# Remainders of the first part's weight tiles: 512 columns by DVE, the other 512 by GpSimd

## The chip, the cores and the metric

The kernel runs on one core of one Trainium2 chip. What is measured is the device time of one execution in microseconds (us). Of the core's engines the text uses these names: PE is TensorE's matmul stream and PEld its weight loads, DVE is VectorE, ACT is ScalarE, POOL is GpSimd, SP is the engine that issues most of the weight loads from memory. Each engine takes its instructions strictly in the order of its queue in this program, and waits on semaphores for the others.

## What is computed

One block of a streaming encoder on 256 tokens of 2048 channels, all in float32. Cut to what matters:

```
h = rmsnorm(x, norm1_g) * (1 + scale1) + shift1          # shift1, scale1, ... = silu(c) @ ada_w + ada_b
proj = h @ w_in                                           # 2048 -> 9216 columns
u, v, q, k, vb, gates = split(proj)
y_a = spatial_gating(gelu(u), gelu(v)) @ w_branch_a       # layer norm, 8 groups of 128 x 128 block-causal mixing
y_b = band_attention(q, k, vb, rel_bias) @ w_branch_b     # 16 heads
x = x + gate1 * ((sig(gates_a) * y_a + sig(gates_b) * y_b) @ w_out)
h = rmsnorm(x, norm2_g) * (1 + scale2) + shift2
x = x + gate2 * moe(h)                                    # 32 SwiGLU experts, top-1 group, top-2 experts in it
out = rmsnorm(x, final_g)
```

The first part is everything up to `w_out`: four dense products with weights (`w_in`, `w_branch_a`, `w_branch_b`, `w_out`). The second part is the 32 experts.

## The kernel before, in words

In the first part the matmuls run on the type fp32r, and precision is kept by splitting each operand in two: a high half, which is the value rounded to fp32r, and a remainder, which is the value less its high half. A product is then three matmuls: high by high, remainder of the activations by high, and high by remainder of the weights.

`run_steps` does that for one stretch of weight columns. It loads weights in pieces of 2 MB (`rw`, tiles r0 to r3) and works on **weight tiles** of 128 rows by `cw` columns (1024, but 512 in the last two stretches of `w_out`). For each weight tile, `prepare` makes the high half on ACT (L315, a cast into `wh`) and then the remainder on DVE (L316, `wl = src - wh`). Both lie in the tile W, which has two slots for high halves and two for remainders, used in turn. `prods` then gives PE the matmuls of that tile: for two token halves and two column halves of 512, L289 (high by high), L290 (activation remainder by `wh`) and L291 (activation high by `wl`), 12 in all. `push` writes the preparation of one tile ahead of the matmuls of the tile before, so that ACT and DVE work one tile ahead of PE. There are 192 weight tiles of 1024 columns and 32 of 512.

Order of the first part: `w_in` in four blocks of four row tiles (`BLOCKS`), each over five stretches of 1024 columns (20 weight tiles a block, `homes`); the partial sums of blocks 2 to 4 are added on DVE (L350, one operand from PSUM). Then the four gate stretches of `w_in` (16 tiles each), with attention and spatial gating as side work between the matmuls; then the branches (8 tiles each, four times); then `w_out` (16 tiles of 1024 columns, and 32 of 512).

Beside this, DVE computes the conditioning vectors without PE: `ada_block` and `ada_units` multiply rows of `ada_w` by a column of silu(c) and add them to an accumulator, one `scalar_tensor_tensor` of 128x1024 for each row tile (L204 in the blocks, L432 later; both inputs lie in SBUF). These steps are drawn by `next(with_ada)` in `prepare` and at each load, so that they stand in DVE's queue between the remainders; below they are the **conditioning steps**. There are 15 in each of the first three blocks' stretches, and 119 of L432 from the fourth block on.

GpSimd has little to do in the first part: a few memsets, loads of small vectors, and two tiny powers of the layer norm (L636). The order on each engine's queue is set by a scheduler, which places the instructions by its own estimates; `pin` marks those of the second part that it must leave in order. The second part streams 402 MB of expert weights through a ring of tiles, among them W, dC, dD and E of the first part.

Of the kernel before, what the change touches and what calls it, by code (L numbers as in the profile page):

```python
# [10 lines left out]
F32 = mybir.dt.float32  # L11
# [34 lines left out]
def hybrid_block(  # L46
# [25 lines left out]
    nc = tc.nc  # L72
# [10 lines left out]
    class Ring:  # L83
# [4 lines left out]
        def next(self):  # L88
            self.i = (self.i + 1) % len(self.tags)
            return self.tags[self.i - 1]  # L90
# [15 lines left out]
    def load(shape, src):  # L106
        t = raws.sb(shape)
        nc.sync.dma_start(out=t, in_=src)
        return t
# [6 lines left out]
    def push(prepare, products):  # L116
        prepare()
        if pending:
            pending.pop()()
        pending.append(products)  # L120
# [7 lines left out]
    def tick():  # L128
        for g in list(sides):
            if next(g, "end") == "end":  # L130
                sides.remove(g)
# [141 lines left out]
    def run_steps(lh, ll, w, k0, n, c0, evac, with_ada=None, cw=CW, after=None):  # L273

        nhf = cw // 512
        npc = 4096 // cw
        pt = []

        def prods(k, wh, wl, close):
            def f():  # L280
                if not pt:
                    pt.extend([bk.ps() for _ in range(nhf)] for _ in range(NT))
                for t in range(NT):
                    a = lh(k)[:, t * P : (t + 1) * P]
                    b = ll(k)[:, t * P : (t + 1) * P]
                    for hf in range(nhf):
                        cs = slice(hf * 512, (hf + 1) * 512)
                        o = pt[t][hf]
                        nc.tensor.matmul(o, a, wh[:, cs], start=(k == k0), stop=False)  # L289
                        nc.tensor.matmul(o, b, wh[:, cs], start=False, stop=False)  # L290
                        nc.tensor.matmul(o, a, wl[:, cs], start=False, stop=close)  # L291
                if close:
                    for t in range(NT):
                        for hf in range(nhf):
                            evac(t, hf, pt[t][hf])
                    if after is not None:
                        after()
                tick()

            return f  # L300

        for q in range(k0, k0 + n, npc):
            m = min(npc, k0 + n - q)
            rw = load([P, m, cw], w[q * P : (q + m) * P, c0 : c0 + cw].rearrange("(j p) n -> p j n", p=P))
            if with_ada is not None:
                next(with_ada, None)
            for jj in range(m):
                k = q + jj
                i2 = nsplit[0] % 2
                nsplit[0] += 1  # L310
                wh = split[:, i2, 0:cw]
                wl = split[:, 2 + i2, 0:cw]

                def prepare(wh=wh, wl=wl, src=rw[:, jj, :]):
                    nc.scalar.copy(wh, src)  # L315
                    nc.vector.tensor_sub(wl, src, wh.bitcast(F32))  # L316
                    if with_ada is not None:
                        next(with_ada, None)

                push(prepare, prods(k, wh, wl, k == k0 + n - 1))  # L320
# [658 lines left out]
    for j in range(-1, 4):  # L979
        for a in range(2):  # L980
            o, cs = pgate[a * CH : (a + 1) * CH, :], slice(a * 512, (a + 1) * 512)
# [570 lines left out]
```

## Time and profile before

| | us |
|---|---|
| median of 3 runs | 1694.18 (1693.98 to 1696.93) |
| the profiled execution, its own time | 1694.83 |
| its span (first to last profiled instruction) | 1693.1 |

| engine | busy, share of the span |
|---|---|
| PE | 1540.7 us, 91% |
| PEld | 858.7 us, 51% |
| DVE | 946.7 us, 56% |
| ACT | 483.5 us, 29% |
| POOL | 125.1 us, 7% |

Two stretches have to be told apart. The first part's weight tiles run on PE from 45 us to 698 us; after that the experts run to the end, with memory traffic near its ceiling throughout. The shares above are means over both. A busy PE says little, since ends of matmuls are modelled; the spacing of the weight tiles and the waits say more.

### The profile page before, as it was taken

What the parts mean: (1) busy time and instruction counts of PE and PEld (TensorE: products, weight loads), DVE (VectorE), ACT (ScalarE), POOL (GpSimd) and SP (SyncE); (2) the same over time, 40 slices, a digit from 0 to 9 for tenths busy, and PEclk for the clock granted to TensorE, in tenths of its full rate; (3) what the DMA queues carried; (4) which work ended last, traced back from release to release, by engine and by line L of the source; (5) the groups of instructions that cost most, each with busy time, mean ns of one, the idle gap of its engine ahead of it and who ended that gap; (6) DMA issues with size and microseconds to landing.
All of it is one profiled execution on the core that took longest, in us unless ns stands there. A gap on an engine that the chain in (4) does not pass through costs nothing. (4 is left out here: it accounts for less than half of the span.)

```text
span 1693.1 us, 18219 instructions
## 1 busy us (share of the span) xinstructions
PE 1540.7 (91%) x6709; PEld 858.7 (51%) x6709; DVE 946.7 (56%) x1320; ACT 483.5 (29%) x785; POOL 125.1 (7%) x377
## 2 busy tenths in 40 slices
PE   2999999999999999899998989989899898898996
PEld 1777778777887776543333323334233243332432
DVE  5789999998778979733432333323333333332334
ACT  4554345675444345331111111111111111111112
POOL 1000000000000000011110101001001010010101
PEclk9999999999999999899999999999999999999998
DMA  9988997797987886979999999999999999999996
GB/s 358 352 314 330 347 341 299 286 348 278 354 314 304 325 320 221 368 311 418 416 417 418 415 418 417 417 417 416 419 417 417 418 416 419 416 417 418 415 420 244
DMA packets 135359, 625.25 MB, mean 369 GB/s; under 512 B 5721, under 2 KB 5841, under 8 KB 101857
## 3 DMA queue, kind: packets, MB, share of 16 engines
q1 hardware_dynamic: 132832, 614.49, 91.3%
q10 hardware_dynamic: 992, 5.28, 0.8%
q0 software_dynamic: 1440, 4.27, 0.8%
q8 instruction: 55, 0.90, 0.2%
q14 instruction: 40, 0.32, 0.0%
HBM read 621.91 MB, written 2.10 MB: 369 GB/s over the span
## 5 line engine op out<-in xcount | busy, mean ns | idle before, releaser
L1203 PE MATMUL b<-r,e 128*64 128x512 f32 x1008 | 372.4, 640 | 43.8 <-DMA r<-in_w_dram 43.7
L1342 DVE TENSOR_TENSOR dB<-dB,b 128x512 f32<-128x512 f32 x248 | 153.6, 681 | 320.1 <-PE b L1340 320.1
L315 ACT CAST W<-r 128x1024 fp32r<-128x1024 f32 (+1 forms) x224 | 220.8, 987 | 326.5 <-PE b L290 291.8
L289 PE MATMUL b<-W,dC 128*128 128x512 f32 x704 | 284.2, 404 | 6.0 <-ACT dC L230 3.7
L316 DVE TENSOR_TENSOR W<-r,W 128x1024 fp32r<-128x1024 f32 (+1 forms) x224 | 255.3, 1145 | 60.5 <-ACT W L315 59.2
L290 PE MATMUL b<-W,dD 128*128 128x512 f32 x704 | 279.5, 397 | 0.0
L291 PE MATMUL b<-W,dC 128*128 128x512 f32 x704 | 266.9, 398 | 2.1 <-DVE W L316 1.9
L1332 ACT CAST f<-f 64x512 fp32r<-64x512 f32 x124 | 76.5, 617 | 578.9 <-DVE dB L1342 416.9
L1203 PEld LDWEIGHTS b<-r,e 128*64 128x64 f32 x1008 | 115.2, 146 | 227.6 <-issue 155.6
L432 DVE SCALAR_TENSOR_TENSOR f<-r,sc,f 128x1024 f32<-128x1024 f32 x119 | 152.2, 1280 | 4.4 <-DMA r<-in_ada_w_dram 3.6
L289 PEld LDWEIGHTS b<-W,dC 128*128 128x128 f32 x704 | 132.5, 188 | 41.5 <-ACT W L315 4.3
L291 PEld LDWEIGHTS b<-W,dC 128*128 128x128 f32 x704 | 131.2, 188 | 38.3 <-DVE W L316 7.1
L290 PEld LDWEIGHTS b<-W,dD 128*128 128x128 f32 x704 | 132.5, 188 | 30.4 <-issue 0.5
L1203 PE MATMUL b<-dC,e 128*64 128x512 f32 x272 | 123.5, 607 | 18.5 <-DMA dC<-in_w_dram 18.4
L1203 PE MATMUL b<-E,e 128*64 128x512 f32 x256 | 120.0, 624 | 20.2 <-DMA E<-in_w_dram 20.2
L1203 PE MATMUL b<-dD,e 128*64 128x512 f32 x256 | 124.8, 637 | 0.0
L1299 DVE TENSOR_TENSOR f2y<-f2y,b 128x256 f32<-128x256 f32 x31 | 13.1, 421 | 196.0 <-ACT f2y L1298 196.0
L1203 PE MATMUL b<-W,e 128*64 128x512 f32 x256 | 118.2, 609 | 0.6 <-POOL e L1216 0.5
L1308 PE MATMUL b<-r,f2y 128*64 128x512 f32 x512 | 114.7, 595 | 2.0 <-DVE f2y L1299 2.0
L1333 DVE TENSOR_TENSOR f<-f,f 64x512 fp32r<-64x512 f32 x124 | 85.1, 686 | 26.4 <-ACT f L1332 23.5
L1218 POOL COPY e<-a 128x64 f32 x256 | 67.5, 267 | 203.7 <-PE b L1203 189.9
L204 DVE SCALAR_TENSOR_TENSOR f<-r,sc,f 128x1024 f32<-128x1024 f32 x60 | 76.9, 1281 | 1.6 <-DMA r<-in_ada_w_dram 1.0
(313 smaller groups left out, 1473.6 us busy)
## 6 DMA issues: line engine op xcount, KB each, us to landing
r<-in_w_dram SPq DMA_DIRECT2D x92, 2048.0 KB, 28.2
r<-in_w_in_dram SPq DMA_DIRECT2D x36, 2048.0 KB, 8.1
r<-in_ada_w_dram SPq DMA_DIRECT2D x32, 2048.0 KB, 8.8
W<-in_w_dram SPq DMA_DIRECT2D x24, 2048.0 KB, 28.1
dC<-in_w_dram SPq DMA_DIRECT2D x23, 2048.0 KB, 28.3
dD<-in_w_dram SPq DMA_DIRECT2D x23, 2048.0 KB, 28.7
E<-in_w_dram SPq DMA_DIRECT2D x23, 2048.0 KB, 28.1
r<-in_ada_w_dram SPq DMA_DIRECT2D x32, 1024.0 KB, 10.1
```

The costliest lines, as they stand in the source:

```text
L204: nc.vector.scalar_tensor_tensor(out=acc, in0=rw[:, jj], scalar=sc[:, j : j + 1], in1=acc, op0=ALU.mult, op1=ALU.add,)
L289: nc.tensor.matmul(o, a, wh[:, cs], start=(k == k0), stop=False)
L290: nc.tensor.matmul(o, b, wh[:, cs], start=False, stop=False)
L291: nc.tensor.matmul(o, a, wl[:, cs], start=False, stop=close)
L315: nc.scalar.copy(wh, src)
L316: nc.vector.tensor_sub(wl, src, wh.bitcast(F32))
L432: nc.vector.scalar_tensor_tensor(out=acc, in0=rw[:, jj, :], scalar=sc[:, j : j + 1], in1=acc, op0=ALU.mult, op1=ALU.add,)
L1203: nc.tensor.matmul(pab[a * CH : (a + 1) * CH, :], xe[:, 8 * half + j, :], w[:, j // JQ, j % JQ, :], start=(half == 0 and j == 0), stop=(ha ...
L1308: nc.tensor.matmul(po[a * CH : (a + 1) * CH, :], act[:, j, :], w[:, j, a * 512 : (a + 1) * 512], start=(j == 0), stop=(j == 3),)
L1332: pin(nc.scalar.copy(oh[r, a, :], og[r, b, :]))
L1333: pin(nc.vector.tensor_sub(oh[o, a, :], og[r, b, :], oh[r, a, :].bitcast(F32)))
L1342: pin(nc.vector.tensor_add(xa[:, t, d0 : d0 + 512], xa[:, t, d0 : d0 + 512], pr))
```

## The change

Of the remainder of a weight tile, DVE keeps the first 512 columns, and GpSimd computes the 512 beside it. Tiles of 512 columns have nothing left for GpSimd.

```
                 def prepare(wh=wh, wl=wl, src=rw[:, jj, :]):
                     nc.scalar.copy(wh, src)
-                    nc.vector.tensor_sub(wl, src, wh.bitcast(F32))
+
+                    for eng, cs in ((nc.gpsimd, slice(512, cw)), (nc.vector, slice(0, 512))):
+                        if cs.start < cw:
+                            eng.tensor_sub(wl[:, cs], src[:, cs], wh[:, cs].bitcast(F32))
                     if with_ada is not None:
                         next(with_ada, None)
```

In the changed program later lines stand three lines lower: L319 is the remainder (L316 before) on either engine, L353 the adding of partial sums (L350 before), L204 is the conditioning step in both. The scheduler places the queues anew. Three places:

**DVE, second block, two stretches of `w_in`.** Before: W is the remainder, f the conditioning step, E and e the adding of partial sums.

```order
L316 TENSOR_TENSOR W_63<-r_86_678,W_63 128x1024
L350 TENSOR_TENSOR E_228<-E_228,b_83_633 128x512
L350 TENSOR_TENSOR E_228<-E_228,b_84_634 128x512
L350 TENSOR_TENSOR E_228<-E_228,b_85_635 128x512
L316 TENSOR_TENSOR W_63<-r_86_678,W_63 128x1024
L204 SCALAR_TENSOR_TENSOR f_80_606<-r_87_680,sc_92,f_80_606 128x1024
L316 TENSOR_TENSOR W_63<-r_86_678,W_63 128x1024
L204 SCALAR_TENSOR_TENSOR f_80_606<-r_87_680,sc_92,f_80_606 128x1024
L316 TENSOR_TENSOR W_63<-r_86_678,W_63 128x1024
L204 SCALAR_TENSOR_TENSOR f_80_606<-r_87_680,sc_92,f_80_606 128x1024
```

The same place in the changed program:

```order
L319 TENSOR_TENSOR W_63<-r_86_702,W_63 128x512
L353 TENSOR_TENSOR E_228<-E_228,b_83_655 128x512
L353 TENSOR_TENSOR E_228<-E_228,b_84_656 128x512
L353 TENSOR_TENSOR E_228<-E_228,b_85_657 128x512
L319 TENSOR_TENSOR W_63<-r_86_702,W_63 128x512
L204 SCALAR_TENSOR_TENSOR f_80_626<-r_87_704,sc_92,f_80_626 128x1024 x2
L319 TENSOR_TENSOR W_63<-r_86_702,W_63 128x512
L204 SCALAR_TENSOR_TENSOR f_80_626<-r_87_704,sc_92,f_80_626 128x1024 x2
L319 TENSOR_TENSOR W_63<-r_86_702,W_63 128x512
```

The remainders are half as wide, and the conditioning steps stand in pairs between two remainders instead of one by one.

**POOL, from the start of the weight tiles.** Before, after the memset L268, come a memset (L400) and small loads of the fourth block:

```order
L241 TENSOR_TENSOR rs_n_21_105<-ve_n_20_103,mhalf_71 128x2
L268 MEMSET f_30_157 64x8x64
L400 MEMSET f_326_2821 128x1024
L401 DMA f_326_2821<-in_ada_b_dram 1x16x64
L498 DMA dB_1378<-in_gmlp_ln_g_dram 128x1024
```

In the changed program:

```order
L241 TENSOR_TENSOR rs_n_21_105<-ve_n_20_103,mhalf_71 128x2
L268 MEMSET f_30_157 64x8x64
L319 TENSOR_TENSOR W_63<-r_46_233,W_63 128x512 x4
L319 TENSOR_TENSOR W_63<-r_53_295,W_63 128x512 x4
L319 TENSOR_TENSOR W_63<-r_59_372,W_63 128x512 x4
L319 TENSOR_TENSOR W_63<-r_65_449,W_63 128x512 x4
```

GpSimd's queue, empty there before, now holds one subtraction of 128x512 for each of the 192 tiles of 1024 columns, and its memsets and loads stand between them.

**PE, third block.** Before, the matmuls of the second weight tile of a stretch: the four that need the remainder (L291) come last.

```order
L289 MATMUL b_121_1092<-W_63,dC_97 128x512
L290 MATMUL b_121_1092<-W_63,dD_98 128x512
L289 MATMUL b_122_1093<-W_63,dC_97 128x512
L290 MATMUL b_122_1093<-W_63,dD_98 128x512
L289 MATMUL b_123_1094<-W_63,dC_97 128x512
L290 MATMUL b_123_1094<-W_63,dD_98 128x512
L289 MATMUL b_124_1095<-W_63,dC_97 128x512
L290 MATMUL b_124_1095<-W_63,dD_98 128x512
L291 MATMUL b_121_1092<-W_63,dC_97 128x512
L291 MATMUL b_122_1093<-W_63,dC_97 128x512
L291 MATMUL b_123_1094<-W_63,dC_97 128x512
L291 MATMUL b_124_1095<-W_63,dC_97 128x512
```

The same tile in the changed program:

```order
L289 MATMUL b_121_1138<-W_63,dC_97 128x512
L290 MATMUL b_121_1138<-W_63,dD_98 128x512
L291 MATMUL b_121_1138<-W_63,dC_97 128x512
L289 MATMUL b_122_1139<-W_63,dC_97 128x512
L290 MATMUL b_122_1139<-W_63,dD_98 128x512
L291 MATMUL b_122_1139<-W_63,dC_97 128x512
L289 MATMUL b_123_1140<-W_63,dC_97 128x512
L290 MATMUL b_123_1140<-W_63,dD_98 128x512
L291 MATMUL b_123_1140<-W_63,dC_97 128x512
L289 MATMUL b_124_1141<-W_63,dC_97 128x512
L290 MATMUL b_124_1141<-W_63,dD_98 128x512
L291 MATMUL b_124_1141<-W_63,dC_97 128x512
```

PE now asks for DVE's half of the remainder at the third matmul of this tile, and for GpSimd's half at the sixth, where before it asked for the whole at the ninth.

## Rows read from the trace of the kernel before

**Rows 1.** Stretches: length, busy us (instructions) PE, PEld, DVE, ACT, POOL; clock, DMA share, GB/s.

```profile
45.00:104.00 59.00, 58.50 (x247) 46.31 (x248) 46.55 (x49) 34.43 (x52) 0.00 (x0) 0.97 0.92 341
104.00:280.00 176.00, 172.77 (x750) 136.97 (x749) 168.99 (x190) 74.57 (x84) 4.11 (x6) 1.00 0.90 336
280.00:401.00 121.00, 121.00 (x630) 92.55 (x629) 110.30 (x164) 80.51 (x172) 10.37 (x25) 1.00 0.80 299
401.00:493.00 92.00, 91.96 (x405) 73.84 (x404) 74.89 (x67) 39.21 (x44) 1.50 (x2) 1.00 0.82 312
493.00:590.00 97.00, 94.36 (x408) 74.38 (x407) 82.96 (x91) 37.26 (x41) 3.05 (x5) 1.00 0.84 320
590.00:639.00 49.00, 48.66 (x213) 37.90 (x212) 37.74 (x40) 19.95 (x23) 0.00 (x0) 1.00 0.82 308
639.00:698.00 59.00, 55.17 (x246) 40.22 (x244) 52.23 (x68) 30.47 (x53) 0.00 (x0) 1.00 0.72 269
750.00:1693.00 943.00, 841.90 (x3586) 323.68 (x3584) 321.57 (x544) 129.19 (x270) 91.70 (x296) 0.96 1.00 409
```

**Rows 2.** Timeline of ACT, third block: start us, us, instruction, idle before and releaser.

```profile
165.29 1.05 ACT L315 CAST W<-r 128x1024 fp32r<-128x1024 f32 x1 [1.75 <-PE b L290]
168.09 1.05 ACT L315 CAST W<-r 128x1024 fp32r<-128x1024 f32 x1 [1.75 <-PE b L290]
```

**Rows 3.** Timeline of DVE, the same place.

```profile
167.35 1.22 DVE L316 TENSOR_TENSOR W<-r,W 128x1024 fp32r<-128x1024 f32 x1
168.49 1.28 DVE L204 SCALAR_TENSOR_TENSOR f<-r,sc,f 128x1024 f32<-128x1024 f32 x1
169.69 1.22 DVE L316 TENSOR_TENSOR W<-r,W 128x1024 fp32r<-128x1024 f32 x1
...
173.15 1.28 DVE L350 TENSOR_TENSOR E<-E,b 128x512 f32<-128x512 f32 x2
```

**Rows 4.** Groups by line and form, DVE and POOL: count, busy us, mean ns, idle before.

```profile
L316 DVE TENSOR_TENSOR W<-r,W 128x1024 fp32r<-128x1024 f32 x192 | 233.7, 1221 | 55.5 <-ACT W L315 54.4 <-PE b L548 0.5 <-PE b L291 0.2
L316 DVE TENSOR_TENSOR W<-r,W 128x512 fp32r<-128x512 f32 x32 | 21.6, 688 | 4.9 <-ACT W L315 4.9
L432 DVE SCALAR_TENSOR_TENSOR f<-r,sc,f 128x1024 f32<-128x1024 f32 x119 | 152.2, 1280 | 4.4 <-DMA r<-in_ada_w_dram 3.6
L1420 POOL TENSOR_TENSOR dD<-dB,dC 128x512 f32<-128x512 f32 x4 | 5.0, 1270 | 66.0 <-DMA dC<-in_final_g_dram 66.0
```

**Rows 5.** Waits between 55 and 700 us: waiter, waited for, us in total, times, longest.

```profile
PEld b L291 <- DVE W L316: 11.4, 23, 2.6
ACT W L315 <- DVE W L316: 7.7, 5, 2.8
PE b L291 <- DVE W L316: 4.6, 6, 2.2
PEld b L289 <- ACT W L315: 4.5, 6, 2.0
```

**Rows 6.** Timeline of POOL at the layer norm's two powers, and at the final multiplications.

```profile
274.47 0.58 POOL L636 TENSOR_TENSOR brs<-brs,mhalf 128x1 f32<-128x1 f32 x1 [55.10 <-DVE brs L635]
...
291.57 1.46 POOL L636 TENSOR_TENSOR brs<-brs,mhalf 128x1 f32<-128x1 f32 x1 [16.53 <-DVE brs L635]
...
1674.34 4.96 POOL L1420 TENSOR_TENSOR dD<-dB,dC 128x512 f32<-128x512 f32 x4 [65.97 <-DMA dC<-in_final_g_dram]
```

**Rows 7.** Timeline of DVE at the same places.

```profile
274.30 0.68 DVE L631 BATCH_NORM_STATS2 bst<-x 128x6 f32<-128x512 f32 x1
...
291.40 1.22 DVE L645 TENSOR_TENSOR x<-x,dB 128x1024 f32<-128x1024 f32 x1
292.61 1.23 DVE L316 TENSOR_TENSOR W<-r,W 128x1024 fp32r<-128x1024 f32 x1
...
1677.21 2.48 DVE L1450 TENSOR_TENSOR dB<-dB,b 128x512 f32<-128x512 f32 x4 [1.22 <-PE b L1445]
```

## The prediction, made before the changed kernel ran

> **What bounds the kernel now.** I read the stretches first [rows 1]. The last row says that from 750 us on the DMA engines are busy all the time (share 1.00, 409 GB/s): the experts run at the speed of memory. Their ring takes over W, dC, dD and E, which the weight tiles hold until their last matmul, so this stretch starts when the first part ends. I therefore pass every microsecond gained or lost in the first part on to the total, and look for the change only between 45 and 639 us (639 to 698 us holds the 512-column tiles, which have nothing for GpSimd).
>
> There, the spacing of the weight tiles is to be read, not PE's busy share. ACT casts a tile every 2.80 us (165.29, 168.09), each time released by PE's L290 of an earlier tile after 1.75 us of idling [rows 2]: PE sets the pace, at 12 matmuls in 2.80 us. 192 tiles of 2.80 us and 32 half ones are 582 us of the 653 us between 45 and 698; the rest is side work of PE (transposes, attention) and a few waits. So PE is the bound, and DVE stands close behind: 169 us busy of 176 between 104 and 280 us, 110 of 121 in the gate stretches with attention, and less after [rows 1]. What DVE's remainder costs now is in the waits: PE's weight loads waited 11.4 us for L316, its matmuls 4.6 us, and another 4.5 us for casts, some of which had waited for the remainder of an older slot (7.7 us on ACT) [rows 5]. More than about 20 us the change can't win in the first part, since nothing else of PE's time depends on the remainder.
>
> **The change, part by part.**
>
> *DVE's half.* A remainder of 1024 columns occupies DVE for 1.14 us (start of L316 to start of the next instruction, 167.35 to 168.49), a conditioning step for 1.20 us [rows 3]. The 512-column form takes 688 ns [rows 4]; two additions of 128x512 take 1.28 us together [rows 3], so such an instruction occupies DVE for 0.60 us. That frees 0.54 us for each of 192 tiles, 104 us of DVE in all, most of it in slack.
>
> *GpSimd's half.* The nearest row is L1420, a tensor_tensor of 128x512 from two SBUF tiles: 1270 ns [rows 4], and four in a row take 4.96 us [rows 6], so 1.23 us each. It writes plain fp32; no row has GpSimd write fp32r. I take 1.23 us, the lowest it can be; the upper end is open, and I put 2 us there. Taken alone it fits: the cast ends 1.1 us into the tile before, GpSimd's half would be there 2.4 us into it, and it is due only at the sixth matmul of its own tile, at 2.8 + 1.2 us.
>
> *What the two do to each other* is the term that decides. L1420 ran beside DVE instructions with one operand in PSUM (L1450 at 1677.21) and was not slowed [rows 6, 7]. The power L636 shows the other case. It took 0.58 us when DVE ran bn_stats, and 1.46 us when it was released 0.17 us after DVE had started L645, which reads two SBUF tiles [rows 6, 7]. It began at 291.57 and ended at 293.03, 0.42 us after L645's end at 292.62: GpSimd could not read until that instruction was through, and then got in ahead of most of the next one. So GpSimd's reads are held by a DVE instruction with two SBUF inputs. L316 and the conditioning steps are exactly of that kind. Does GpSimd hold DVE in turn? The power reads one element a partition, and the L316 behind it took 1.23 us, as always [rows 7]: this trace has no long GpSimd read in front of such a DVE instruction. The bounds are 0 and the whole 1.23 us for each tile. I take the whole, by symmetry with the power's hold, which lasted until the DVE instruction was done.
>
> The Trainium skill has a rule on this, which speaks against the change (SBUF — State Buffer, section "Who interferes with whom"): DVE's second read port is shared with GpSimd, a DVE instruction with two SBUF inputs contends with a GpSimd instruction that reads SBUF, and whichever comes second waits until the first is done. On GpSimd's side the trace agrees (1.46 us in place of 0.58); on DVE's side no run here shows it yet. By that rule the cost below stands; without it the faster rival does.
>
> *The sum, with DVE held.* Then a tile costs DVE and GpSimd together 0.60 + 1.23 in place of 1.14 us, 0.69 us more, and where their work comes one after the other a stretch can't be shorter than its DVE time plus that [rows 1]:
> - 45 to 104 us, 20 tiles: 46.6 + 13.8 = 60.4, against 59: +1.4.
> - 104 to 280 us, 60 tiles: 169.0 + 41.4 = 210.4, against 176: +34.4.
> - 280 to 401 us, 32 tiles: 110.3 + 22.1 = 132.4, against 121: +11.4.
> - 401 to 493 us, 32 tiles: 74.9 + 22.1 = 97.0, against 92: +5.0.
> - 493 to 590 us, 32 tiles: 83.0 + 22.1 = 105.1, against 97: +8.1.
> - 590 to 639 us, 16 tiles: 37.7 + 11.0 = 48.7, against 49: 0.
>
> That is +60. Against it, DVE instructions with a PSUM operand (60 additions L350 between 104 and 280 us, 36 us) can run beside GpSimd. If all of that hid, the stretch would need only its two-input work: 60 × (0.60 + 1.23) + 45 steps × 1.20 = 164 of 176 us, and nothing would be lost. So I walked through four tiles of the second block in the new order (remainder, two steps, remainder, two steps, remainder), GpSimd served after each DVE instruction as the power was. PE starts tile 0 at 0. Tile 1 is cast at 1.1: GpSimd to 2.3, DVE's half to 2.9, due at 3.3: in time. First step to 4.1; tile 2 was cast at 3.9, so GpSimd goes next, to 5.3; second step to 6.5, DVE's half to 7.1, due at 5.6 + 0.5: 1.0 us late, and PE, which now asks for it at its third matmul, stands. Tile 3 starts at 9.4 and is cast at 6.7: GpSimd to 8.3, two steps to 10.7, DVE's half to 11.3, due at 9.9: 1.4 us late. That is 2.4 us in four tiles, 36 us in 60, about the serial 34.4. So in that stretch I take the serial value whole. In the two stretches with much PSUM work besides (280 to 401, 493 to 590) I take half, 6 and 4. With 1.4 and 5.0 the sum is +51 us. The waits that the change was to remove are inside the stretches' lengths and aren't taken off again. In the blocks and gates the pacing goes over from PE to the pair of DVE and GpSimd.
>
> *GpSimd's queue.* Memsets and loads that wait for others now have remainders behind them: the memsets of the score tiles, eight pairs, wait for DVE (and DVE's maximum waits for them, now behind a remainder), L636 waits for DVE, the memset L400 for PE's transposes. All are in program order with what they wait for; I put them at nothing, because DVE's own remainder, in order behind the same work, covers them, and at one GpSimd instruction (1.23 us) for some ten of them, 12 us, if not.
>
> *PE's order.* Nothing is added to PE. Its earlier asking costs nothing alone, it only makes lateness show.
>
> **The rivals.**
> 1. *DVE isn't held* (the faster side). GpSimd waits for a gap, DVE never waits. The point from which it decides: a conditioning step with a GpSimd subtraction inside it still takes 1.28 us. Then DVE's half is early everywhere, and the waits for L316 go: 11.4 + 4.6 = 16 us, up to 20.5 with the casts: 1674 to 1679, or half of that, about 1686, where GpSimd is late itself. For it: no row shows DVE held. Against: GpSimd is.
> 2. *It packs* (no change). DVE is held, but PSUM work and PE's slack take it up, as the 164 of 176 us allow: within 3 us of 1694. Against: DVE's queue is in order, and the walk found no such place.
> 3. *GpSimd's half is dearer* (2 us, as fp32r output or hand-overs might make it). Then 0.77 us more on 160 to 176 tiles, some of it covered: another 40 to 80 us, 1780 and above.
> 4. *The change does nothing for GpSimd* in 32 of the 224 tiles (512 columns); that is in the sum. The others it splits, as the queues show.
>
> **How the numbers follow.** The profiled execution took 1694.83 us, the median is 1694.18, so a sum made on the one holds for the other within a microsecond. Forecast, DVE held: +51, so 1745, with 1705 (most of the PSUM work hidden) to 1775 (all serial, and the queue's 12 us): chance 0.64. Rival 1: 0.18. Rival 2: 0.08. Rival 3: 0.10. About 0.2% (3.4 us) is what a measurement of this kernel tells from no change. Faster by more has rival 1, 0.18; within it 0.08; slower the forecast and rival 3, 0.74. The range goes from 1684, which takes in the weaker half of rival 1, to 1790, the lower part of rival 3.
>
> **What would show it right or wrong.** Right: conditioning steps and 512-column remainders on DVE with a mean well over 1.28 and 0.69 us, tiles of the second to fourth block spaced by 3.2 us or more, waits of L291 for DVE's L319 above 11 us, and POOL's L319 often over 1.27 us. Wrong: L204 and L432 still at 1.28 us (rival 1); DVE held, but the blocks still at 58 us each (rival 2); POOL's L319 at 1.7 us or more even where DVE is idle (rival 3); or a second part that doesn't begin later by what the first part lost.

## The result, and the profile of the changed kernel

The changed kernel took 1780.87 us (median of 4 runs, 1778.63 to 1781.1) against 1694.08 us for the kernel before in the same comparison: ratio 1.0509, 95% interval 1.0494 to 1.0524. It is 87 us slower; the forecast was 51 us slower, with a range up to 1790. The profiled execution took 1780.93 us, its span 1779.2 us. The weight tiles on PE run from 45 to 788 us where they ran to 698, so the first part lost 90 us, and nearly all of it passed on to the total.

First the stretches of the changed kernel, cut at the same places of the program as [rows 1]: length, busy us (instructions) of PE, PEld, DVE, ACT, POOL, then granted clock, DMA share, GB/s.

```profile
45.00:116.00 71.00, 62.61 (x249) 47.39 (x250) 50.46 (x49) 35.35 (x54) 31.77 (x19) 0.95 0.80 298
116.00:327.00 211.00, 183.76 (x750) 139.92 (x749) 184.18 (x191) 74.19 (x84) 97.53 (x66) 0.97 0.74 275
327.00:462.00 135.00, 127.08 (x627) 93.55 (x626) 109.60 (x162) 80.88 (x171) 60.34 (x57) 0.99 0.71 263
462.00:569.00 107.00, 95.77 (x404) 73.81 (x403) 82.55 (x70) 38.81 (x44) 55.03 (x34) 0.98 0.73 275
569.00:677.00 108.00, 98.79 (x408) 76.25 (x407) 85.67 (x92) 37.64 (x40) 55.56 (x38) 0.97 0.81 310
677.00:730.00 53.00, 49.94 (x214) 37.85 (x214) 37.94 (x39) 19.99 (x23) 26.45 (x15) 1.00 0.64 237
730.00:788.00 58.00, 55.72 (x246) 39.65 (x244) 51.04 (x68) 30.37 (x53) 0.00 (x0) 1.00 0.66 250
```

Every stretch with a GpSimd half is longer; the last, which has none, is not. DVE, whose remainders were halved, is busier than before in five of the seven rows (184.2 us against 169.0 in the second).

Why, the groups by line and form show (first part; count, busy us, mean ns, idle before). L319 is the remainder, L204 and L435 (L432 before) the conditioning steps, L353 the adding of partial sums (L350 before), L202 the first step of an accumulator.

```profile
L319 POOL TENSOR_TENSOR W<-r,W 128x512 fp32r<-128x512 f32 x190 | 308.3, 1625 | 336.9 <-ACT W L315 322.9 <-PE b L291 7.0 <-PE b L551 5.7
L319 DVE TENSOR_TENSOR W<-r,W 128x512 fp32r<-128x512 f32 x222 | 193.9, 879 | 104.7 <-ACT W L315 104.4
L435 DVE SCALAR_TENSOR_TENSOR f<-r,sc,f 128x1024 f32<-128x1024 f32 x119 | 193.3, 1624 | 7.1 <-DMA r<-in_ada_w_dram 6.0
L204 DVE SCALAR_TENSOR_TENSOR f<-r,sc,f 128x1024 f32<-128x1024 f32 x45 | 87.6, 1947 | 0.6
L353 DVE TENSOR_TENSOR E<-E,b 128x512 f32<-128x512 f32 x24 | 15.4, 681 | 2.9 <-PE b L291 2.9
L202 DVE TENSOR_SCALAR f<-r,sc 128x1024 f32<-128x1024 f32 x3 | 4.4, 1467 | 0.0
```

The same instructions that took 1280 ns before [rows 4] now take 1624 and 1947 in the mean; the remainder of 512 columns took 688 and takes 879 in the mean, the 32 tiles without a GpSimd half included. The additions with an operand in PSUM are not touched: 681 ns, and 679 where both halves are on DVE (below). On DVE's whole busy time: the narrower remainders freed 192 × (1221 − 688) = 102 us [rows 4], and yet it rose from 946.7 to 975.2 us. So DVE was held for 102 + 28.5 = 131 us, 0.68 us for each GpSimd subtraction. The relief was more than eaten.

One hold can be watched whole, in the third block. Timeline of DVE, then of POOL: start us, us, instruction, idle before and releaser.

```profile
188.05 0.68 DVE L319 TENSOR_TENSOR W<-r,W 128x512 fp32r<-128x512 f32 x1
188.65 2.32 DVE L204 SCALAR_TENSOR_TENSOR f<-r,sc,f 128x1024 f32<-128x1024 f32 x1
190.89 0.68 DVE L319 TENSOR_TENSOR W<-r,W 128x512 fp32r<-128x512 f32 x1
191.49 3.52 DVE L204 SCALAR_TENSOR_TENSOR f<-r,sc,f 128x1024 f32<-128x1024 f32 x2
194.93 0.68 DVE L319 TENSOR_TENSOR W<-r,W 128x512 fp32r<-128x512 f32 x1
```

```profile
188.47 1.41 POOL L319 TENSOR_TENSOR W<-r,W 128x512 fp32r<-128x512 f32 x1 [1.50 <-ACT W L315]
192.35 1.57 POOL L319 TENSOR_TENSOR W<-r,W 128x512 fp32r<-128x512 f32 x1 [2.47 <-ACT W L315]
```

The subtraction that began at 188.47 ended at 189.88; the step begun at 188.65 ended at 190.97, 1.09 us after that, where a step takes 1.28 us in all [rows 3]: nearly the whole step came only when GpSimd was through. The next subtraction began at 192.35, inside the first step of a pair begun at 191.49. Taking the first step at its usual 1.20 us, that step ended at 192.69; the subtraction then needs its 1.23 us [rows 6] and ends at 193.92, as it does; the second step ends at 195.01, 1.09 us later. Whoever comes second waits until the other is done, in both directions.

What PE pays is in the waits between 45 and 790 us (us in total, times, longest):

```profile
PEld b L291 <- DVE W L319: 66.3, 62, 4.5
PE b L291 <- DVE W L319: 43.6, 37, 4.0
ACT W L315 <- POOL W L319: 15.1, 9, 1.9
PEld b L291 <- POOL W L319: 6.7, 9, 1.6
```

Before, the first two were 11.4 and 4.6 us [rows 5]. PE waits for DVE's half, hardly for GpSimd's; the casts wait 15.1 us for a slot that GpSimd has still to read.

### The profile page after: what moved, and what is told of

It reads as the page before. It is cut to its first block, busy times and chain, and to the rows that moved or that the text cites. A ratio compares the mean times of both kernels' runs of the same rounds, so it can differ in the third digit from the quotient of the medians.

```text
span 1779.2 us, 18510 instructions
## 1 busy us (share of the span) xinstructions
PE 1565.0 (88%) x6709; PEld 862.9 (49%) x6709; DVE 975.2 (55%) x1320; ACT 484.3 (27%) x785; POOL 435.6 (24%) x569
## 4 chain that ended last, share of the span: by engine, by line
DMA 40%; PE 31%; DVE 20%; issue 5%; ACT 2%; POOL 1%; SPq 0%; POOLq 0%; ACTq 0%; DVEq 0%
DMA r<-in_w_dram 22%; PE b L1206 11%; DMA dC<-in_w_dram 8%; DMA E<-in_w_dram 8%; DVE f L435 6%; PE b L291 5%; DVE W L319 5%; PE b L289 4%; PE b L290 4%; DVE f L204 4%; PE b L1311 2%; DMA r<-in_ada_w_dram 2%; ACT W L315 1%; POOL W L319 1%; DMA r<-in_w_out_dram 1%
## 5 line engine op out<-in xcount | busy, mean ns | idle before, releaser
L1206 PE MATMUL b<-r,e 128*64 128x512 f32 x1008 | 367.2, 629 | 44.3 <-DMA r<-in_w_dram 44.3
L319 POOL TENSOR_TENSOR W<-r,W 128x512 fp32r<-128x512 f32 x192 | 311.4, 1624 | 344.2 <-ACT W L315 330.2
L291 PE MATMUL b<-W,dC 128*128 128x512 f32 x704 | 287.3, 411 | 38.2 <-DVE W L319 35.1
L289 PE MATMUL b<-W,dC 128*128 128x512 f32 x704 | 288.2, 410 | 7.8 <-ACT dC L230 4.0
L319 DVE TENSOR_TENSOR W<-r,W 128x512 fp32r<-128x512 f32 x224 | 196.3, 883 | 104.7 <-ACT W L315 104.4
L435 DVE SCALAR_TENSOR_TENSOR f<-r,sc,f 128x1024 f32<-128x1024 f32 x119 | 193.3, 1624 | 7.1 <-DMA r<-in_ada_w_dram 6.0
L291 PEld LDWEIGHTS b<-W,dC 128*128 128x128 f32 x704 | 134.5, 192 | 90.7 <-DVE W L319 54.3
L1219 POOL COPY e<-x 128x256 f32 x64 | 25.5, 401 | 603.8 <-PE b L1206 579.3
L289 PEld LDWEIGHTS b<-W,dC 128*128 128x128 f32 x704 | 135.1, 192 | 43.0 <-ACT W L315 6.1
```

What stands on the lines that cost most here:

```text
L319: eng.tensor_sub(wl[:, cs], src[:, cs], wh[:, cs].bitcast(F32))
L435: nc.vector.scalar_tensor_tensor(out=acc, in0=rw[:, jj, :], scalar=sc[:, j : j + 1], in1=acc, op0=ALU.mult, op1=ALU.add,)
L1206: nc.tensor.matmul(pab[a * CH : (a + 1) * CH, :], xe[:, 8 * half + j, :], w[:, j // JQ, j % JQ, :], start=(half == 0 and j == 0), stop=(ha ...
```

## The experiments

The theory was A, contention: the two engines hold each other at SBUF. Its rivals were B, that GpSimd's half itself comes late, and C, that the split and the new order of the queues cost the time without any contention.

**Both halves on DVE.** The split and the order of writing stay, GpSimd is out of it.

```
-for eng, cs in ((nc.gpsimd, slice(512, cw)), (nc.vector, slice(0, 512))):
+for eng, cs in ((nc.vector, slice(512, cw)), (nc.vector, slice(0, 512))):
```

> The changed kernel with both halves of the remainder on DVE, GpSimd left out. Theory A (GpSimd and DVE hold each other at the shared read port): close to the kernel before. Two 512-column instructions occupy DVE 0.06 us longer than one of 1024; in the 60 tiles where DVE is full that is 4 us, so 1694 to 1702. Theory C (the new order, with steps in pairs and PE asking for the first half earlier, costs the time by itself): well above, 1720 or more.

Measured: 1697.59 us against 1693.66, ratio 1.0022 (1.0013 to 1.0032). The split costs at most 4 us of the 87. The order of the queues this run doesn't test: the scheduler placed them anew here too, and up to the fourth block its conditioning steps stand between two remainders as 40 single ones, one pair and one three, where the changed kernel has 12 single ones, 12 pairs and 3 threes. Its loss lies in the fourth block, which took 66.5 us where it took 59.4 before.

**An idle subtraction.** The kernel before, with a GpSimd subtraction of 128x512 in each of the 80 tiles of the blocks, into a tile that nobody reads; DVE does its whole remainder.

```
 nc.vector.tensor_sub(wl, src, wh.bitcast(F32))
+if n == 4:
+    nc.gpsimd.tensor_sub(spare[0], src[:, 512:CW], wh[:, 512:CW].bitcast(F32))
```

> The kernel before, DVE computing the whole remainder, and in the 80 tiles of the four blocks GpSimd subtracts the second 512 columns as well, into a spare tile that nobody reads. Nobody waits for GpSimd's result. Theory A: DVE is held 1.23 us a tile on top of all its work: 71 us in place of 59 in the first block, 243 in place of 176 in the next three, so up to +79, 1735 to 1775, with conditioning steps far above 1.28 us. Theory B (only lateness of GpSimd's half counts, DVE isn't held): 1694. Theory C: 1694.

Measured: 1745.14 us, ratio 1.0302 (1.0281 to 1.0322), 51 us slower. Its stretch of the blocks, and the groups in it (L318 is the idle subtraction, L316 the remainder):

```profile
45.00:332.00 287.00, 245.91 (x998) 181.64 (x998) 276.00 (x237) 110.28 (x137) 149.29 (x84) 0.99 0.74 275
```

```profile
L316 DVE TENSOR_TENSOR W<-r,W 128x1024 fp32r<-128x1024 f32 x190 | 260.0, 1372 | 49.3 <-ACT W L315 47.1 <-PE b L290 0.6 <-PE b L552 0.5
L318 POOL TENSOR_TENSOR a<-r,W 128x512 fp32r<-128x512 f32 x78 | 145.1, 1861 | 132.0 <-ACT W L315 98.8 <-issue 30.3 <-DVE sh L220 2.4
L204 DVE SCALAR_TENSOR_TENSOR f<-r,sc,f 128x1024 f32<-128x1024 f32 x45 | 78.8, 1752 | 0.2
```

The blocks take 287 us where they took 59 + 176 = 235 [rows 1]: all of the loss lies where the subtraction runs, and it is no less than the 47 us that the changed kernel lost there (71 + 211 − 235). No data of GpSimd's is asked for (three casts waited for its reads, 6.1 us in all), so contention alone does it: A is shown, and B isn't needed here. Nor is C: up to the fourth block the steps stand in DVE's queue as in the kernel before (27 single ones, 6 pairs, 2 threes in both), and the remainder isn't split.

**A write only.** The kernel before, with a GpSimd memset of the remainder's slot in the same 80 tiles, ahead of the remainder. It writes 128x1024 and reads nothing.

```
+if n == 4:
+    nc.gpsimd.memset(wl.bitcast(F32), 0.0)
 nc.vector.tensor_sub(wl, src, wh.bitcast(F32))
```

> The kernel before, and in the 80 tiles of the four blocks GpSimd fills the remainder's slot with zeros (128x1024, 0.96 us, writes only) before DVE writes the remainder there. Theory A (reads of GpSimd and DVE hold each other): 1692 to 1699. If any GpSimd work beside DVE held it: 0.96 us in 80 tiles, 50 us or more as the idle subtraction cost, 1735 to 1745.

Measured: 1700.07 us, ratio 1.0039 (1.0025 to 1.0053), 6.8 us slower, 1 us above the range that was expected.

```profile
L318 DVE TENSOR_TENSOR W<-r,W 128x1024 fp32r<-128x1024 f32 x190 | 231.4, 1220 | 61.2 <-ACT W L315 46.1 <-POOL W L317 13.9 <-PE b L550 0.5
L317 POOL MEMSET W<- 128x1024 f32 x78 | 75.1, 962 | 166.4 <-PE b L291 155.4 <-DVE W L318 5.3 <-DVE f L202 2.0
L204 DVE SCALAR_TENSOR_TENSOR f<-r,sc,f 128x1024 f32<-128x1024 f32 x45 | 57.6, 1279 | 0.2
```

Remainder and steps keep their 1220 and 1279 ns; those that ran beside a memset took no more (remainders up to 1225, steps up to 1290 ns). The first three blocks took 176.5 us, as before (175.9). The loss lies in the fourth, which took 66.3 us in place of 59.4, nearly as with both halves on DVE (66.5), where GpSimd has no part in the remainder; how much of it is the new placement was not settled. The remainder's waits for the memset ahead of it (13.9 us in all) are for the slot that both write. So it is GpSimd's reads that hold DVE's instructions with two SBUF inputs. A tensor_scalar, with one, was held by a memset as well: the one below took 1.23 us, and the same instruction 0.81 at 295.48 us, where no memset ran; a memset stood beside it from 279.50 to 280.45.

```profile
279.76 1.23 DVE L640 TENSOR_SCALAR x<-x,bmv,brs 128x1024 f32<-128x1024 f32 x1
```

**Without the conditioning steps.** The accumulating steps are left out of both kernels (the first step of each accumulator stays, and the loads). The cut shows the blocks; the later steps go in the same way.

```
     if j == 0:
         ...
-    else:
-        nc.vector.scalar_tensor_tensor(
-            out=acc, in0=rw[:, jj], scalar=sc[:, j : j + 1], in1=acc,
-            op0=ALU.mult, op1=ALU.add,
-        )
```

The kernel before without them:

> The kernel before without the conditioning steps after the first of each accumulator (164 instructions of 1.28 us beside the weight tiles left out, so the conditioning vectors are not those of the reference); loads and all else stay. All theories: DVE has room, its waits go: 1674 to 1690. It is the base for the next.

The changed kernel without them:

> The changed kernel, the same conditioning steps left out. Theory A: the two-input work at the port is 0.60 + 1.23 us a tile against 2.80 us on PE, so the loss nearly goes: within 8 us of the kernel before without steps. Theory B (GpSimd's half is late by itself, or its queue is): most of the 87 us stays.

Measured: 1696.16 us for the first, ratio 1.0019 (1.0008 to 1.0029), where at least 4 us of gain was expected, and 1715.78 us for the second, ratio 1.0128 (1.0108 to 1.0148), 20 us above the first where at most 8 was expected. Both missed. Busy time of the engines, first kernel, then second:

```profile
PE 1538.4 (91%) x6709; PEld 862.9 (51%) x6709; DVE 741.4 (44%) x1141; ACT 483.0 (29%) x785; POOL 124.2 (7%) x377
```

```profile
PE 1552.5 (91%) x6709; PEld 855.2 (50%) x6709; DVE 681.7 (40%) x1141; ACT 483.6 (28%) x785; POOL 449.9 (26%) x569
```

The first showed nothing to win: 205 us less on DVE, and no microsecond gained. The waits of PE and PEld for DVE's remainder fell from 16.0 [rows 5] to 5.1 us, but others stand there now, between 45 and 790 us:

```profile
PEld b L284 <- ACT W L310: 15.5, 13, 3.1
PE b L284 <- ACT W L310: 10.5, 8, 2.8
ACT W L310 <- DMA r<-in_w_out_dram: 7.0, 1, 7.0
```

L284 is the first matmul of a tile (L289 before), L310 the cast. PE now waits for casts at the starts of stretches. The one that waited for the load cost it 2.83 us. The four other long waits, at 79.72, 92.80, 152.02 and 211.10 us, cost 1.5 to 1.6 us each, and each time ACT was not waiting: it did other work directly before the cast (copies of partial sums, L343, in the first two, L222 in the others, which had itself waited 4.62 us for DVE). So the scheduler's new placement may hide a gain of some microseconds; that a free DVE is worth nothing is shown for this placement alone.

The second says that 67 of the 87 us need the steps (86.8 − 19.6). Here DVE fell by 741.4 − 681.7 = 60 us, of the 102 freed; 43 us were held, 0.22 us for each subtraction where it was 0.68 with the steps. The last two gate stretches come to 45.7 us each without steps in both kernels, with 27 of 32 tiles at 2.80 us. Of the 20 us that stay, some 10 are lost in the blocks and 6 in the two gate stretches with attention, with DVE busy for 284 of the 605 us from 45 to 650. A part of them is of theory B's kind: PE now waits for GpSimd's half too, and casts for its slots.

```profile
ACT W L310 <- POOL W L314: 23.4, 14, 2.2
PEld b L286 <- POOL W L314: 10.4, 15, 1.1
```

But this half isn't late by itself: its median is 1.81 us, and 1.31 us is what it took once where DVE was idle.

**The order of the steps.** In the changed kernel, the steps of the first three blocks are tied behind DVE's half of their tile (`sub`), which was to take the pairs apart (cut to what matters).

```
-next(with_ada, None)
+with tc.issue_after(sub.ins):
+    next(with_ada, None)
```

> The changed kernel; in the first three blocks' stretches a conditioning step may not be placed ahead of the remainder that it follows in the program, so that DVE's queue alternates remainder and step instead of two steps in a row. Same work on the port. Theory A alone (throughput of the port): these 60 tiles stay as long as in the changed kernel, 209 us against 176 before. Theory A with order (the hold costs where two steps stand in a row and GpSimd gets between them, so that DVE's half is late): by the walk 3.0 us a tile in place of 3.5, 185 to 195 us, in all 1757 to 1768.

Measured: 1779.55 us, ratio 1.0506 (1.0485 to 1.0527). From the first weight tile to the fourth block it takes 206.8 us, in the changed kernel 208.8, in the kernel before 176. But the edit did less than it was meant to. Two steps of different tiles can still stand behind one remainder, and in these blocks 8 of the 12 pairs and all 3 threes are left, for example:

```profile
211.91 4.62 DVE L204 SCALAR_TENSOR_TENSOR f<-r,sc,f 128x1024 f32<-128x1024 f32 x2
216.45 0.68 DVE L320 TENSOR_TENSOR W<-r,W 128x512 fp32r<-128x512 f32 x1
217.05 3.63 DVE L204 SCALAR_TENSOR_TENSOR f<-r,sc,f 128x1024 f32<-128x1024 f32 x2
```

So this run says little about the pairs. That they aren't needed for the loss is shown by the idle subtraction, which lost 52 us with the 6 pairs of the kernel before; what they add in the changed kernel stays open.

**A narrower share.** 256 columns on GpSimd, 768 on DVE; then the same with the steps tied behind.

```
-for eng, cs in ((nc.gpsimd, slice(512, cw)), (nc.vector, slice(0, 512))):
+for eng, cs in ((nc.gpsimd, slice(768, cw)), (nc.vector, slice(0, min(768, cw)))):
```

> The changed kernel with 256 columns on GpSimd and 768 on DVE. Theory A: about 0.65 us of GpSimd and 0.87 of DVE a tile, with a step 2.7 us at the port against 2.80 on PE, so the loss falls to half or less: 1700 to 1735. If the cost is one of handing over (one wait for each tile whatever its width), it stays near 1780.

> 256 columns on GpSimd and steps kept behind their remainder in the first three blocks. If something is to be won by relieving DVE, it is here: 2.7 us at the port against 2.80 on PE. Theory A with order: 1695 to 1715; a version better than the kernel before (under 1690) only if DVE's relief is worth anything, which the kernel without steps speaks against.

Measured: 1723.41 us, ratio 1.0175 (1.0154 to 1.0195), and 1724.75 us, ratio 1.0179 (1.0162 to 1.0196). Half the columns, a third of the loss. The second missed its 1695 to 1715; its tie left 11 of 13 pairs standing, so it too says little about the order. The first one's remainder on either engine, min/median/max in ns:

```profile
L319 DVE TENSOR_TENSOR W<-r,W x224: 679/958/1524, 40.7 to 728.1; 128x768 fp32r<-128x768 f32 x96, 128x512 fp32r<-128x512 f32 x16
L319 POOL TENSOR_TENSOR W<-r,W x192: 725/1517/2320, 39.2 to 667.5; 128x256 fp32r<-128x256 f32 x192
```

A GpSimd subtraction of 256 columns can take 725 ns, but its median is 1517: the rest is waiting for the DVE instruction in front of it, which its own width doesn't shorten. DVE's busy time (954.1 us) stands 7 us over that of the kernel before, and yet the kernel is 30 us slower. No share that was tried beats the kernel before.

## Why the forecast was right, and where it fell short

**DVE is held: right**, and with it the direction. The step taken by symmetry with the power L636 [rows 6] holds: 2.32 us for a step that a subtraction preceded. The Trainium skill's rule (SBUF — State Buffer, section "Who interferes with whom"), that whichever of the two comes second waits until the first is done, agrees in both directions, and so does its remark that a GpSimd instruction that only writes doesn't contend with one of two SBUF inputs (1279 ns with the memsets). The same section counts tensor_scalar among the instructions that can take the shared port; the trace agrees there too, with L202 at 1.80 and 1.85 us where a subtraction ran beside it in the changed kernel and 0.75 where none did, and I had left it out of the sum (3 instructions in the blocks, some 2 us).

**The signs named in advance** came: steps at 1.62 and 1.95 us, DVE's remainder at 0.88, GpSimd's at 1.62, waits for DVE's L319 at 66.3 and 43.6 us, and tiles of the second to fourth block 3.5 us apart (211 / 60). Rival 1 (steps still 1.28 us) and rival 2 (no change) fall by them. Rival 3 reached the right size of time by the wrong cause: a GpSimd half that nothing held takes 1261 ns, so writing fp32r isn't dearer than the 1270 of [rows 4]. Its sign, 1.7 us or more even where DVE is idle, didn't come: the three subtractions beside an idle DVE took 1261 to 1303 ns. That the measured time lies in the stated range is in part luck: it is 6 us above the 1705 to 1775 that I gave the hold of DVE, and only rival 3, which was wrong, took the range up to 1790. The subtractions of the changed kernel (min/median/max ns):

```profile
L319 POOL TENSOR_TENSOR W<-r,W x192: 1261/1718/2369, 39.3 to 725.7; 128x512 fp32r<-128x512 f32 x192
```

**The sum by stretches** is where it fell short (lengths from the rows above and [rows 1], us):

| stretch before | before | after | lost | forecast | all serial |
|---|---|---|---|---|---|
| 45 to 104 | 59 | 71 | 12 | 1.4 | 1.4 |
| 104 to 280 | 176 | 211 | 35 | 34.4 | 34.4 |
| 280 to 401 | 121 | 135 | 14 | 6 | 11.4 |
| 401 to 493 | 92 | 107 | 15 | 5.0 | 5.0 |
| 493 to 590 | 97 | 108 | 11 | 4 | 8.1 |
| 590 to 639 | 49 | 53 | 4 | 0 | 0 |
| 639 to 698 | 59 | 58 | −1 | 0 | 0 |

The failing step is "a stretch can't be shorter than its DVE time plus that": true as a lower bound, but I took it, or half of it, as the length. That suits a stretch in which DVE never idles. Outside the second row DVE idled before, and it still idles after; over the whole first part its idle time before the remainder rose from 60 us (55.5 and 4.9 in [rows 4]) to 104.7. As I read it, time lost to a hold is not made up in that slack, since W has two slots and DVE's queue is in order: DVE waits for a cast, then is held with steps in front of the next remainder, then PE waits. The last gate stretches show the turn. DVE, then POOL:

```profile
473.59 0.69 DVE L319 TENSOR_TENSOR W<-r,W 128x512 fp32r<-128x512 f32 x1 [1.47 <-ACT W L315]
474.20 0.68 DVE L685 TENSOR_TENSOR E<-b,E 128x512 fp32r<-128x512 f32 x1
474.80 3.05 DVE L435 SCALAR_TENSOR_TENSOR f<-r,sc,f 128x1024 f32<-128x1024 f32 x2
477.77 1.80 DVE L319 TENSOR_TENSOR W<-r,W 128x512 fp32r<-128x512 f32 x1
```

```profile
473.64 1.81 POOL L319 TENSOR_TENSOR W<-r,W 128x512 fp32r<-128x512 f32 x1 [5.66 <-ACT W L315]
476.87 2.14 POOL L319 TENSOR_TENSOR W<-r,W 128x512 fp32r<-128x512 f32 x1 [1.43 <-ACT W L315]
479.67 2.25 POOL L319 TENSOR_TENSOR W<-r,W 128x512 fp32r<-128x512 f32 x1 [0.66 <-ACT W L315]
```

DVE idles 1.47 us for the cast; then two steps take 3.05 us, since the subtraction of 473.64 to 475.45 holds the first, and the remainder behind them 1.80 in place of 0.68, since that of 476.87 to 479.01 runs into it; the matmul that needs it comes at 479.62, 0.46 us late. In that stretch DVE was busy 77% of the time, and 15 us were lost. The changed kernel without steps says the same on the whole: DVE less than half busy there, and 20 us lost. That this local lateness explains the excess is read from these places and not shown; no run takes it away alone.

**The second row is right in size by luck.** 60 subtractions were to hold DVE for 1.23 us each. DVE would have needed 169.0 − 60 × 0.54 = 136.6 us and shows 184.2, so it was held for 48 us, 0.8 each; the other 27 us of the 211 DVE was idle, against 7 before. The walk, which gave 2.4 us in four tiles, was too severe on the hold, and the pairs of steps that it blamed aren't needed for such a loss, as the idle subtraction shows. Nor need all 35 us be the hold: the fourth block, the last third of this row, took 7 us more in both runs above that lost time there without a hold by GpSimd's reads (66.5 and 66.3 us for 59.4), and 72.8 in the changed kernel.

**The half** that I let hide in the two stretches with PSUM work was wrong as well: they lost 14 and 11 us, more than the whole serial 11.4 and 8.1. The additions with a PSUM operand aren't held, but they seldom stood beside the subtractions: in the whole changed kernel four of the 192 ran beside nothing else.

**"More than about 20 us the change can't win"** holds as a bound, but no run found anything of it: with 205 us less on DVE the kernel before took 2.5 us longer. PE did not get the waits of [rows 5] back, since casts came late in their place, in the order that the scheduler chose there.

**GpSimd's queue at nothing**: right as far as PE's waits tell (its loads waited 6.7 us for POOL's half); but casts waited 15.1 us for slots that GpSimd had still to read, a wait that the sum had no term for. **First part to total, one to one**: right, 90 us lost by 788 us and 87 in the total.

**PE's order** changed less than the tile shown for it says: before, PE asked for the remainder at the third, sixth, ninth and twelfth matmul in 141 of the 192 tiles already, in the changed kernel in 175. Its earlier asking was not tested alone; the idle subtraction, with PE's order of the kernel before in the first three blocks, lost 37 us in these.

## What to carry to other kernels

Before work of DVE is handed to GpSimd, look at what both read: if GpSimd reads SBUF while DVE runs instructions with two SBUF inputs, each holds the other for whole instructions, and the hold (here 0.68 us for each subtraction) can exceed what was handed over (0.53 us). Test it with an idle copy of the moved instruction beside the unchanged kernel, which prices the contention before anything is moved; and test the prize by leaving DVE's load out, which here gave no gain. After each such run look at the queues again: the scheduler places them anew, and an edit to the order may not do what it was written for. In this kernel, with buffers two deep and queues in order, a mean busy share of 47 to 77% was no promise of slack.

## What was not expected of the hardware

PE's clock fell after some of these waits, which no term of the sum held. PE at a wait for the remainder, and then the granted clock around it (columns as in the table of stretches):

```profile
226.19 0.80 PE L291 MATMUL b<-W,dC 128*128 128x512 f32 x1 [2.20 <-DVE W L319]
226.78 0.63 PE L289 MATMUL b<-W,dC 128*128 128x512 f32 x1
227.21 0.63 PE L290 MATMUL b<-W,dD 128*128 128x512 f32 x1
...
230.13 0.40 PE L289 MATMUL b<-W,dC 128*128 128x512 f32 x1
230.36 0.40 PE L290 MATMUL b<-W,dD 128*128 128x512 f32 x1
```

```profile
226.10:229.60 3.50, 3.41 (x8) 2.77 (x9) 1.23 (x3) 0.12 (x1) 0.00 (x0) 0.51 1.03 418
229.60:233.00 3.40, 3.40 (x16) 2.71 (x16) 2.44 (x2) 1.69 (x2) 1.81 (x1) 1.00 0.79 314
```

After 2.20 us of idling PE ran at the lower level (0.51, 1.2 GHz): matmuls 0.43 us apart; from 229.6 us on, at the higher one (1.00, 2.4 GHz), 0.23 us apart. The eight matmuls took some 1.6 us more than they would have. So a wait can cost more than its length. Not each does: 3.48 us of idling ahead of the matmul at 241.47 us left the granted clock at 1.00 from 241 to 245. As an estimate from the clock column of the stretches, length times what is missing to 1.00 adds up to 17 us in the changed kernel (3.6 + 6.3 + 1.4 + 2.1 + 3.2), and to 2 us before [rows 1]: up to 15 of the 90 us, less what of it fell into waits. No run took the clock's part away by itself, but the loss doesn't rest on it: the idle subtraction lost its 52 us at a mean granted clock of 0.99, where the same stretches had 0.97 and 1.00 before.
